# Cross-attention of a hybrid decoder step: the query layout moved ahead of the prompt scores, and a second prompt output product moved behind the exponential

## The chip, the cores and the metric

One core of one Trainium2 chip runs the whole kernel as one program. The metric is the device time of one execution in microseconds (us); of several runs the median is shown. Engines are named as the profile names them: PE is TensorE's matrix products, PEld its weight loads, DVE is VectorE, ACT is ScalarE, POOL is GpSimd, SP is SyncE. A "q" behind an engine's name means its queue of DMA issues.

## The reference

One inference step of one layer: two recurrent branches (SSD and GLA) merged by gates, cross-attention into 256 memory tokens, and a convolutional FFN. The same weights serve one prompt of 256 tokens and a group of 8 samples with 4 tokens each. All is float32. The change lies in the cross-attention:

```python
def _cross_attend(hn, mem_k, mem_v, w_cq, w_co):
    Bsz, L, _ = hn.shape
    q = (hn @ w_cq).reshape(Bsz, L, CROSS_HEADS, CROSS_HEAD_DIM).astype(jnp.float32)
    s = jnp.einsum('blhd,bmhd->bhlm', q, mem_k.astype(jnp.float32)) * (CROSS_HEAD_DIM ** -0.5)
    pr = jax.nn.softmax(s, axis=-1)
    o = jnp.einsum('bhlm,bmhd->blhd', pr, mem_v.astype(jnp.float32)).astype(hn.dtype)
    return o.reshape(Bsz, L, D_MODEL) @ w_co
```

There are 4 heads of 512 channels. The prompt (one row of 256 tokens) attends to keys and values that the kernel made earlier; each of the 8 samples attends to its own cached 256 keys and values per head.

## The kernel before

Activations stand transposed: 128 channels on the partitions, 288 tokens (256 of the prompt, 32 of the samples) along the free axis. Every weight matrix is loaded in pieces and split into a high and a low part: `whi` by ACT (L98), `wlo` by DVE (L100). Each product of full precision is then three products (high by high, high by low, low by high: L150, L151, L154). A **step** of a projection takes two blocks of 128 input channels and 256 output channels: one `whi`, one `wlo` and 12 products. Five pairs of `whi` and `wlo` are buffered, so ACT and DVE make them up to five steps ahead of PE.

The cross-attention is woven from two generators (L1591 to L1593). The main one is the query projection of the **next** head, 16 steps (`q_proj`, L1386); for the last head it is 12 steps of the output projection `w_co`. The other one is `attend(hd)` (L1430), the attention of the present head, cut into pieces by `yield`. `weave(main, bg, n_main, n_bg)` (L175) writes one main step, then so many pieces of `attend` that after main step i, counted from 0, `(i+1)*25//16` pieces have been written (`(i+1)*25//12` for the last head); what is left of `attend` after the last main step is written at once (`run(bg)`, L183). `attend` has 25 pieces. Through the text, "step 5" is the main step with i=5.

The pieces of `attend` in order, with their line numbers:

1. and 2. two times: four turns of the prompt's keys on PE (L1380), then their split into `kTh` (ACT, L190) and `kTl` (DVE, L191)
3. and 4. two times: `prompt_scores` (12 products of `qh`, `ql` by `kTh`, `kTl`: L1454, L1455, L1456), the prompt's softmax (L1359 to L1364), and two `turn`s of the samples' keys (`kT` from `kc`, DVE, L1419)
5. issue of the other four key loads (`keys`, POOL, L1405); the query layout: 16 products with the identity that spread the samples' queries `qsm` (L1493), and 8 copies on ACT into `xq` (L1498)
6. the split of the prompt's values into `vph` (ACT) and `vpl` (DVE)
7. and 8. sample scores of the first four samples (`la` from `kT`, `xq`, L1446), two times 64 products
9. turns of the prompt's probabilities (L1510), their split, one `turn`
10. to 13. three `turn`s, and behind them the prompt output products 0, 1 and 2 (`prompt_out`, six products each, L1468 to L1470, split into `co`)
14. and 15. issue of the value loads, and the sample scores of the other four samples
16. to 18. the maximum over the samples' scores (L1531 to L1544), and the exponential on ACT (`pu`, L1548)
19. prompt output product 3
20. the sums of the exponentials (L1553) and the probabilities (`rs`, `pu`, DVE, L1368 and L1370)
21. their turns on PE (L1558) and the copies into `pms` (DVE, L1560)
22. and 23. sample outputs, in two halves of 16 products (L1568): first those that read `vc`, then those that read `vq`
24. the copy `os` (ACT, L1572)
25. the products that sum the `os` rows by sample (L1576) and the split into `co`

Loads of cached keys and values and of the prompt's keys and values go through POOL's queue (`cache`, L1402): each is issued behind the one before it, and waits until the third before it has landed. Keys, late values and the prompt's keys and values share five buffers (`x4`, L1323), so the first keys `kc` of a head can be loaded only when the sample outputs of the head before have read its `vc`. A `turn` is placed behind the last `wlo` that has been written when it is written (L1418).

The order of writing is a priority, not the order on an engine: a planner places each instruction on its engine when it takes it to be ready, by its own estimates, earliest written first. The order on each engine is then fixed in the program. So a turn `kT` can be placed ahead of work that was written earlier, and main products stand between two products of `attend`.

Of the kernel before, what the change touches and what calls it, by code (L numbers as in the profile page):

```python
# [20 lines left out]
NB = 8  # L21
# [19 lines left out]
def hybrid_step(ctx: ExitStack, tc: tile.TileContext, I: dict, O: list):  # L41
# [14 lines left out]
    def acc_tile():  # L56
        return ps.tile([P, 512], F32, tag="acc", bufs=4, name="acc")

    def mm_tile():
        return ps.tile([P, 512], F32, tag="mm", bufs=3, name="mm")  # L60
# [128 lines left out]
    def split(hi, lo, src):  # L189
        S.copy(hi, src)  # L190
        V.tensor_tensor(lo, src, hi, ALU.subtract)  # L191
# [1133 lines left out]
    def k4(name):  # L1325
        return px.tile([P, 4, 256], F32, tag="k4", bufs=4, name=name)

    def r4(name):
        return px.tile([P, 4, 256], F32R, tag="r4", bufs=2, name=name)
# [4 lines left out]
    def v2(name):  # L1334
        return r4(name).rearrange("p d m -> p (d m)").rearrange("p (m d) -> p m d", m=2)
# [21 lines left out]
    def softmax(src, n, out):  # L1357
        mx = px.tile([P, 1], F32, tag="mx", bufs=3, name="mx")
        V.tensor_reduce(mx[0:n], src, axis=AX.X, op=ALU.max)  # L1359
        V.tensor_scalar(mx[0:n], mx[0:n], -SC, None, ALU.mult)  # L1360
        sm = px.tile([P, 1], F32, tag="sm", bufs=3, name="sm")
        S.activation(out, src, ACT.Exp, scale=SC, bias=mx[0:n], accum_out=sm[0:n])
        V.reciprocal(sm[0:n], sm[0:n])
        V.tensor_scalar(out, out, sm[0:n], None, ALU.mult)  # L1364
# [9 lines left out]
    def transpose_half(kv, d2):  # L1374

        a = mm_tile()
        for d in range(2):
            for m in range(2):
                dd = 2 * d2 + d
                TR(a[:, d * 256 + m * P:d * 256 + (m + 1) * P], kv[:, m, dd * P:(dd + 1) * P], ident)  # L1380
        return a.rearrange("p (d m) -> p d m", m=256)
# [29 lines left out]
    def rows_of(src, spread=False):  # L1411
        t = x4("kc" if spread else "vc")
        cache(t, src.rearrange("(p m) d -> p m d" if spread else "(m p) d -> p m d", p=P))
        return t

    def turn(kc):
        t = k4("kT").rearrange("p d m -> p (d m)")
        with tc.issue_after(last_lo[0].ins):  # L1418
            V.transpose(t, kc.rearrange("p s d -> p (s d)"))  # L1419
        return t.rearrange("p (s x c) -> p x s c", s=2, c=32)  # L1420

    def keys(hd, b):
        return rows_of(I["cache_mem_k"][b, :, hd, :], True)
# [6 lines left out]
    def attend(hd):  # L1430
# [3 lines left out]
        kc, kT, vc = [], [], []  # L1434
# [14 lines left out]
        def prompt_scores(l):  # L1449
            a = mm_tile()  # L1450
            ls = slice(l * P, (l + 1) * P)
            for d in range(4):
                qh, ql = (x[:, d % 2, ls] for x in qps[hd][d // 2])
                MM(a[:, 0:256], qh, kh[:, d, :], start=(d == 0), stop=False)  # L1454
                MM(a[:, 0:256], qh, kl[:, d, :], start=False, stop=False)  # L1455
                MM(a[:, 0:256], ql, kh[:, d, :], start=False, stop=(d == 3))  # L1456
            return a

        def prompt_softmax(a):
            pp = px.tile([P, 256], F32, tag="prp", bufs=2, name="prp")  # L1460
            softmax(a[:, 0:256], P, pp)
            return pp

        def prompt_out(d):
            a = mm_tile()
            ds_ = slice(d * P, (d + 1) * P)
            for m in range(2):
                MM(a[:, 0:SEQ], vh[:, m, ds_], pTh[:, m, :], start=(m == 0), stop=False)  # L1468
                MM(a[:, 0:SEQ], vh[:, m, ds_], pTl[:, m, :], start=False, stop=False)
                MM(a[:, 0:SEQ], vl[:, m, ds_], pTh[:, m, :], start=False, stop=(m == 1))  # L1470
            split(*(x[:, 0:SEQ] for x in co(4 * hd + d)), a[:, 0:SEQ])
# [6 lines left out]
        for d2 in range(2):  # L1478
            a = transpose_half(kp, d2)
            split(kh[:, 2 * d2:2 * d2 + 2, :], kl[:, 2 * d2:2 * d2 + 2, :], a)  # L1480
            yield
        prs = []
        for l in range(2):
            a = prompt_scores(l)
            prs.append(prompt_softmax(a))
            kT += [turn(kc[2 * l]), turn(kc[2 * l + 1])]
            yield
        for b in range(4, NB):
            kc.append(keys(hd, b))
        a = mm_tile()  # L1490
        for e in range(4):
            for i in (3, 2, 1, 0):
# [2 lines left out]
        for i in range(4):  # L1495
            r = slice(32 * i, 32 * i + 32)
            for q in range(2):
                S.copy(xq[r, :, :, 32 * q + 4 * i:32 * q + 4 * i + 4],  # L1498
                       a[r].rearrange("p (x q j l) -> p q x j l", q=2, j=4, l=NL)[:, q])
        yield  # L1500
        vh, vl = v2("vph"), v2("vpl")
        split(vh, vl, vp)
        yield
# [3 lines left out]
        a = mm_tile()  # L1507
# [8 lines left out]
        for d in range(3):  # L1516
            kT.append(turn(kc[5 + d]))
            yield
            prompt_out(d)
        yield  # L1520
        for b in range(4, NB):
            vals(b)
# [4 lines left out]
        for half in range(2):  # L1527
# [19 lines left out]
        su = px.tile([P, 1], F32, tag="sm", bufs=3, name="su")  # L1547
        S.activation(pu.rearrange("p (c s) -> p s c", s=2), ssc[:, 0:64].rearrange("p (s c) -> p s c", s=2), ACT.Exp,  # L1548
                     scale=SC, bias=mb, accum_out=su)
        yield  # L1550
        prompt_out(3)
        yield
# [3 lines left out]
        a = mm_tile()  # L1556
# [17 lines left out]
        a = mm_tile()  # L1574
# [16 lines left out]
    for hd in range(4):  # L1591
        main = q_proj(hd + 1) if hd < 3 else chain(steps(wo[0], 6), steps(wo[1], 6))
        weave(main, attend(hd), 16 if hd < 3 else 12, 25)  # L1593
# [164 lines left out]
    a = acc_tile()  # L1758
    fr = pf.tile([P, 3], F32, name="fr")
    b = acc_tile()  # L1760
# [65 lines left out]
```

## Time and profile before

| | |
|---|---|
| median of 3 runs | 2580.44 us (2579.44 to 2588.53) |
| profiled execution | 2577.89 us, span of its instructions 2576.1 us |
| granted TensorE clock, mean | 0.997 |
| PE busy | 2549.1 us (99%) |
| PEld busy | 2452.3 us (95%) |
| DVE busy | 1710.9 us (66%) |
| ACT busy | 1362.2 us (53%) |
| POOL busy | 298.7 us (12%) |
| DMA | 527.70 MB, mean 205 GB/s |

PE is busy nearly throughout, but this busy time is modelled: products overlap in it, and a stretch in which PE waits shows only as idle time in front of an instruction. So single waits are read from the lists of waits and from the instructions in order of time, not from the share. The cross-attention with its woven projections runs from about 1447 to 1636 us of the span, 47 to 50 us for each of the first three heads, 43.5 us for the last.

### The profile page before, as it was taken

The page shows a single profiled execution, that of the slowest core. Times are in us where ns is not written, and L with a number is a line of the kernel's source. Part 1 is how long each engine was busy: PE and PEld are TensorE (multiplying, and loading weights), DVE is VectorE, ACT ScalarE, POOL GpSimd, SP SyncE. Part 2 cuts the span into 40 slices and gives each one's busy share as a digit, 9 for nine tenths or more (in the row PEclk, how much of TensorE's full clock was granted, in tenths as well). Part 3 has the DMA queues.
Part 4 walks back from the last instruction along what each step waited for, and adds up shares of the span by engine and source line. Part 5 has one row for each costly group of instructions (what it writes and reads, how often), then busy time and mean ns, then how long its engine had stood idle before and what let it go on. Part 6 is the DMA issues. An engine that isn't in the chain of part 4 may idle for free. (4 is left out here: it accounts for less than half of the span.)

```text
span 2576.1 us, 51724 instructions
## 1 busy us (share of the span) xinstructions
PE 2549.1 (99%) x19781; PEld 2452.3 (95%) x19781; DVE 1710.9 (66%) x3647; ACT 1362.2 (53%) x2785; POOL 298.7 (12%) x388
## 2 busy tenths in 40 slices
PE   9999999999999999999999999999999999999998
PEld 7889999999999999999999988999999999999998
DVE  6656778667656666566676656567767576675765
ACT  7655566556553545454555534455545454454545
POOL 2002000000000000000110222202202021120200
PEclk9999999999999999999999999999999999999999
DMA  8666666766477857676876788845555555555553
GB/s 269 207 224 204 201 199 189 214 202 210 150 246 242 261 182 249 206 241 215 274 237 206 258 292 273 248 156 164 164 168 171 168 161 170 169 161 181 170 169 127
DMA packets 456724, 527.70 MB, mean 205 GB/s; under 512 B 23384, under 2 KB 401672, under 8 KB 456412
## 3 DMA queue, kind: packets, MB, share of 16 engines
q1 hardware_dynamic: 432780, 444.89, 53.9%
q0 software_dynamic: 23424, 79.24, 9.3%
q8 instruction: 155, 2.54, 0.4%
q14 instruction: 93, 0.76, 0.1%
q10 hardware_dynamic: 272, 0.26, 0.0%
HBM read 472.05 MB, written 52.26 MB: 204 GB/s over the span
## 5 line engine op out<-in xcount | busy, mean ns | idle before, releaser
L98 ACT CAST whi<-raw 128x512 fp32r<-128x512 f32 (+1 forms) x1464 | 897.2, 618 | 1039.5 <-PE acc L151 790.8
L100 DVE TENSOR_TENSOR wlo<-raw,whi 128x512 fp32r<-128x512 f32 (+1 forms) x1464 | 988.0, 687 | 686.3 <-ACT whi L98 666.6
L150 PE MATMUL acc<-xn,whi 128*128 128x288 f32 (+1 forms) x1936 | 552.1, 300 | 0.0
L151 PE MATMUL acc<-xn,whi 128*128 128x288 f32 (+1 forms) x1936 | 540.4, 295 | 0.0
L154 PE MATMUL acc<-xn,wlo 128*128 128x288 f32 (+1 forms) x1936 | 412.2, 294 | 0.1
L151 PE MATMUL acc<-hf,whi 128*128 128x288 f32 x1408 | 394.5, 296 | 0.0
L150 PE MATMUL acc<-hf,whi 128*128 128x288 f32 x1408 | 393.7, 294 | 0.0
L150 PEld LDWEIGHTS acc<-xn,whi 128*128 128x128 f32 (+1 forms) x1936 | 363.7, 188 | 11.8 <-issue 8.3
L151 PEld LDWEIGHTS acc<-xn,whi 128*128 128x128 f32 (+1 forms) x1936 | 364.1, 188 | 4.0 <-issue 2.9
L154 PEld LDWEIGHTS acc<-xn,wlo 128*128 128x128 f32 (+1 forms) x1936 | 310.1, 188 | 0.7 <-DVE wlo L100 0.6
L154 PE MATMUL acc<-hf,wlo 128*128 128x288 f32 x1408 | 298.5, 293 | 0.0
L151 PEld LDWEIGHTS acc<-hf,whi 128*128 128x128 f32 x1408 | 265.1, 188 | 0.0
L150 PEld LDWEIGHTS acc<-hf,whi 128*128 128x128 f32 x1408 | 264.6, 188 | 0.0
L154 PEld LDWEIGHTS acc<-hf,wlo 128*128 128x128 f32 x1408 | 226.0, 188 | 0.0
L1645 POOL COPY fsp<-fst 128x16 f32<-128x16 f32 x88 | 126.3, 1437 | 664.2 <-ACT fca L1651 366.7
L150 PE MATMUL acc<-pr,whi 128*128 128x288 f32 x704 | 196.8, 295 | 0.8 <-ACT whi L98 0.8
L151 PE MATMUL acc<-pr,whi 128*128 128x288 f32 x704 | 196.9, 295 | 0.0
L154 PE MATMUL acc<-pr,wlo 128*128 128x288 f32 x704 | 148.7, 292 | 0.0
L150 PE MATMUL acc<-un,whi 128*128 128x288 f32 x512 | 147.7, 304 | 0.1
L151 PE MATMUL acc<-un,whi 128*128 128x288 f32 x512 | 143.0, 295 | 0.0
L150 PEld LDWEIGHTS acc<-pr,whi 128*128 128x128 f32 x704 | 132.2, 188 | 1.0 <-ACT whi L98 1.0
L151 PEld LDWEIGHTS acc<-pr,whi 128*128 128x128 f32 x704 | 132.4, 188 | 0.0
(544 smaller groups left out, 4146.9 us busy)
## 6 DMA issues: line engine op xcount, KB each, us to landing
raw<-in_w_in_dram SPq DMA_DIRECT2D x240, 512.0 KB
raw<-in_w_up_dram SPq DMA_DIRECT2D x176, 512.0 KB
raw<-in_w_down_dram SPq DMA_DIRECT2D x88, 512.0 KB
raw<-in_w_cv_dram SPq DMA_DIRECT2D x32, 512.0 KB
raw<-in_w_ssd_out_dram SPq DMA_DIRECT2D x32, 512.0 KB
sin<-in_state_gla_dram POOLq DMA_DIRECT2D x32, 512.0 KB, 5.6
out_dram<-sin SPq DMA_DIRECT2D x32, 512.0 KB
raw<-in_w_gla_out_dram SPq DMA_DIRECT2D x32, 512.0 KB
```

The costliest lines, as they stand in the source:

```text
L98: S.copy(hi, raw)
L100: last_lo[0] = V.tensor_tensor(lo, raw, hi, ALU.subtract)
L150: MM(a, hi[:, k, cs], xh, start=(k0 + s0 + k == 0), stop=False)
L151: MM(a, hi[:, k, cs], xl, start=False, stop=False)
L154: MM(a, lo[:, k, cs], xh, start=False, stop=(k0 + s0 + k == nk - 1))
L1645: G.tensor_copy(sp[:, :, 0:2], st.rearrange("p (b k) -> p b k", k=2))
```

## The change

Two moves in `attend`; no instruction is added or taken away.

The query layout (the former piece 5 without the key loads) is written before the two prompt scores, as piece 3, so it stands between the turns of the prompt's keys and the prompt scores. Both prompt scores with their softmax and their turns of sample keys become pieces 4 and 5. The four key loads open the piece of the value split.

Prompt output product 2 is taken out of the loop and written behind the exponential, just ahead of product 3, with a `yield` of its own between exponential and product. The piece that held product 2 is now empty, so `attend` has 26 pieces, while `n_bg` stays 25: the 26th is written by `run(bg)`.

By the formula of `weave` the pieces then fall to the main steps as follows (heads 0 to 2):

| written behind main step | before | after |
|---|---|---|
| 0 | key turns 0 | key turns 0 |
| 1 | key turns 1, prompt scores 0 | key turns 1, query layout |
| 2 | prompt scores 1 | prompt scores 0 |
| 3 | query layout, value split | prompt scores 1, value split |
| 4 to 6 | sample scores, probabilities' turns | the same |
| 7 | output products 0 and 1 | output products 0 and 1 |
| 8 | output product 2, sample scores | sample scores |
| 9 to 11 | sample scores, maximum, exponential | the same |
| 12 | output product 3, sums | output products 2 and 3 |
| 13 | turns of the probabilities | sums |
| 14 | both halves of the sample outputs | turns of the probabilities, first half of the sample outputs |
| 15 | `os`, sums by sample | second half, `os`, sums by sample |

For the last head (12 main steps) the prompt scores 0 stand behind step 1 in both, now with the query layout ahead of them; prompt scores 1 move from step 1 to 2; sums and turns of the probabilities stand together behind step 10, and all of the sample outputs, `os` and the sums by sample behind step 11.

```diff
             a = transpose_half(kp, d2)
             split(kh[:, 2 * d2:2 * d2 + 2, :], kl[:, 2 * d2:2 * d2 + 2, :], a)
             yield
-        prs = []
-        for l in range(2):
-            a = prompt_scores(l)
-            prs.append(prompt_softmax(a))
-            kT += [turn(kc[2 * l]), turn(kc[2 * l + 1])]
-            yield
-        for b in range(4, NB):
-            kc.append(keys(hd, b))
         a = mm_tile()
         for e in range(4):
             for i in (3, 2, 1, 0):
...
                 S.copy(xq[r, :, :, 32 * q + 4 * i:32 * q + 4 * i + 4],
                        a[r].rearrange("p (x q j l) -> p q x j l", q=2, j=4, l=NL)[:, q])
         yield
+        prs = []
+        for l in range(2):
+            a = prompt_scores(l)
+            prs.append(prompt_softmax(a))
+            kT += [turn(kc[2 * l]), turn(kc[2 * l + 1])]
+            yield
+        for b in range(4, NB):
+            kc.append(keys(hd, b))
         vh, vl = v2("vph"), v2("vpl")
         split(vh, vl, vp)
         yield
...
         for d in range(3):
             kT.append(turn(kc[5 + d]))
             yield
-            prompt_out(d)
+            if d < 2:
+                prompt_out(d)
         yield
...
                      scale=SC, bias=mb, accum_out=su)
+        yield
+        prompt_out(2)
         yield
         prompt_out(3)
         yield
```

## The prediction

> **What bounds the kernel now.** I read the page first, then the waits of PE and its weight loads in the stage of the cross-attention, then the waits of DVE and ACT there, then the instructions in order of time around one border between heads.
>
> ```profile
> span 2576.1 us, 51724 instructions
> PE 2549.1 (99%) x19781; PEld 2452.3 (95%) x19781; DVE 1710.9 (66%) x3647; ACT 1362.2 (53%) x2785; POOL 298.7 (12%) x388
> ```
>
> PE bounds the kernel. A change that neither adds nor removes a product can only move the time by the waits of PE. So the question is how much PE waits in this stage (1425 to 1640 us), and for whom. The list of waits, weight loads first, then one row of the products; the columns are total us, times, longest:
>
> ```profile
> PEld mm L1454 <- ACT kTh L190: 5.0, 3, 2.0
> PEld mm L1455 <- DVE kTl L191: 4.4, 4, 1.2
> PEld mm L1553 <- ACT pu L1548: 1.8, 2, 1.7
> PEld mm L1576 <- ACT os L1572: 1.6, 1, 1.6
> PEld la L1446 <- ACT xq L1498: 1.0, 3, 0.3
> ...
> PE la L1446 <- ACT xq L1498: 1.7, 1, 1.7
> ```
>
> The prompt scores wait 5.0 + 4.4 = 9.4 us for the split of the prompt's keys, the sample scores 1.0 + 1.7 = 2.7 us for the query layout, the sums of the exponentials 1.8 us for the exponential. These 13.9 us, 0.54% of 2577.9, are what the change can reach.
>
> Why the split is late shows at the border from head 0 to head 1 (PE, POOL, DVE, ACT in order of time; start, length, and in brackets the idle time before it and who ended it):
>
> ```profile
> 1488.64 1.93 PE L1568 MATMUL la<-vc,pms 128*32 128x512 f32 x16
> 1490.38 1.90 PE L1568 MATMUL la<-vq,pms 128*32 128x512 f32 x16
> 1493.91 0.97 PE L1576 MATMUL mm<-fold,os 128*128 128x32 f32 x8
> 1496.38 0.60 PE L1380 MATMUL mm<-ident,vc 128*128 128x128 f32 x4
> 1498.39 0.60 PE L1380 MATMUL mm<-ident,vc 128*128 128x128 f32 x4
> 1500.79 0.39 PE L1454 MATMUL mm<-kTh,qh 128*128 128x256 f32 x1 [1.79 <-ACT kTh L190]
> 1502.17 0.39 PE L1455 MATMUL mm<-kTl,qh 128*128 128x256 f32 x1 [1.00 <-DVE kTl L191]
> 1508.39 1.08 PE L1493 MATMUL mm<-qsm,ident 128*32 128x128 f32 x32
> ...
> 1490.85 2.16 POOL L1405 DMA_DIRECT2D kc<-in_cache_mem_k_dram  x3 [6.61 <-PE la L1568]
> 1497.84 0.72 POOL L1405 DMA_DIRECT2D kc<-in_cache_mem_k_dram  x1 [4.83 <-DMA kc<-in_cache_mem_k_dram]
> ...
> 1489.19 0.69 DVE L100 TENSOR_TENSOR wlo<-raw,whi 128x512 fp32r<-128x512 f32 x1 [0.76 <-ACT whi L98]
> 1497.31 1.25 DVE L1419 STREAM_TRANSPOSE kT<-kc 128x1024 f32<-128x1024 f32 x1 [7.43 <-DMA kc<-in_cache_mem_k_dram]
> 1498.48 0.38 DVE L1395 TENSOR_TENSOR qs<-acc,rstd 128x256 f32<-128x256 f32 x1
> 1500.31 1.23 DVE L1419 STREAM_TRANSPOSE kT<-kc 128x1024 f32<-128x1024 f32 x1
> 1501.47 0.65 DVE L191 TENSOR_TENSOR kTl<-mm,kTh 128x512 fp32r<-128x512 f32 x1
> 1502.05 1.22 DVE L1419 STREAM_TRANSPOSE kT<-kc 128x1024 f32<-128x1024 f32 x1
> 1503.19 0.65 DVE L191 TENSOR_TENSOR kTl<-mm,kTh 128x512 fp32r<-128x512 f32 x1
> 1503.77 1.22 DVE L1419 STREAM_TRANSPOSE kT<-kc 128x1024 f32<-128x1024 f32 x1
> ...
> 1498.90 0.83 ACT L190 CAST qh<-qs 128x256 fp32r<-128x256 f32 x2 [3.71 <-DVE qs L1395]
> ```
>
> The chain: the first half of the sample outputs frees the buffers (1490.6), POOL issues the new keys (1490.85), the first lands 6.5 us later; its turn `kT` was placed on DVE ahead of the query scaling `qs` and holds DVE for 7.43 us. So `qs` is late, behind it `qh` on ACT, behind that `kTh`; and a second turn stands ahead of `kTl`. It is the same at all three borders:
>
> ```profile
> DVE kT L1419 <- DMA kc<-in_cache_mem_k_dram: 20.4, 3, 7.4
> ACT qh L190 <- DVE qs L1395: 11.3, 4, 3.7
> ```
>
> **The change part by part.**
>
> *Prompt scores behind the layout.* A main step is about 1.6 us: the two starts of L1380 are 2.0 us apart, less four turns for which I take 0.4. Between the second key turns and the prompt scores there now lie the layout (1.08 us) and one more step, 2.7 us. In head 0, whose keys are loaded early, only `kTl` is waited for; I take a quarter of 4.4, 1.1 us, and it goes: **-1.1**. The other three borders hold 9.4 - 1.1 = 8.3 us, 2.8 each.
>
> There the sample outputs move as well. The first half now has to wait for `pms`, and half a main step can be placed ahead of it, so the last `qs` become ready before the new keys are even asked for; I expect `qs` and `qh` ahead of the turn. I count from the issue of the first key (t = 0). PE leaves the first half at t = -0.3; then half a step 0.8, second half 1.8, step 0 1.6, sums by sample 0.8, turns 0.4, step 1 1.6, turns 0.4, layout 1.1, step 2 1.6: the prompt scores could start at t = 9.8. DVE gets the first key at 6.5. If three turns (1.2 each) stand ahead of the first `kTl` (0.65), it is done at 10.8 and 1.0 to 1.1 us of waiting are left; the second `kTl`, 11.4, comes just as the products that need it do. If only one or two turns stand ahead, nothing is left. If the fourth turn stands ahead of the second `kTl`, much is left (the second rival). I take 1.1 for each border, nearest to the row order in which turns and `kTl` alternate but with DVE free earlier: 8.3 - 3.3, **-5.0** (ends -8.3 and +5).
>
> *Layout earlier.* Its copies on ACT:
>
> ```profile
> 1460.88 0.62 ACT L98 CAST whi<-raw 128x512 fp32r<-128x512 f32 x1 [2.21 <-DMA raw<-in_w_cq_dram]
> 1461.41 2.55 ACT L1498 COPY xq<-mm 32x256 f32<-32x256 f32 x8
> ```
>
> They take 2.55 us, and in head 0 stood behind a `whi` that waited for a weight load. Now two prompt scores and two more steps lie between layout and sample scores. **-2.7** (ends -2.7 and 0). The copies now stand on ACT ahead of the exponentials of the prompt's softmax; those follow the prompt scores, a step later than the layout, so nothing waits.
>
> *Two products behind the exponential.* The 1.8 us come nearly all from the end of head 2:
>
> ```profile
> 1581.07 0.62 ACT L98 CAST whi<-raw 128x512 fp32r<-128x512 f32 x1 [4.53 <-DMA raw<-in_w_co_dram]
> 1581.59 0.31 ACT L1548 ACTIVATE pu<-la,mb 128x64 f32<-128x64 f32 x1
> ...
> 1582.04 0.38 PE L1553 MATMUL mm<-su,total 128*128 128x1 f32 x2 [1.46 <-ACT pu L1548]
> ```
>
> The sums now come a whole step (1.6 us) and six products later: **-1.8** (ends -1.8 and 0, if the weight load is later by as much). The place that product 2 leaves needs no cover: nothing waited there.
>
> *Everything behind it is a piece later.* Turns of the probabilities and first half of the sample outputs now stand together in heads 0 to 2, as they do now in the last head:
>
> ```profile
> 1627.69 0.38 PE L1558 MATMUL mm<-ident,pu 128*128 128x128 f32 x2
> 1628.80 1.92 PE L1568 MATMUL la<-vc,pms 128*32 128x512 f32 x16
> ...
> 1628.11 0.49 DVE L1560 COPY pms<-mm 128x128 f32<-128x128 f32 x2 [0.90 <-PE mm L1558]
> ```
>
> From turns to outputs 1.1 us pass, 0.9 without the turns themselves, and in this row no wait is left because half a main step stands between. I take 0.1 a head, **+0.3** (ends 0.3 and 2.7). In the last head no main product is left at that place: **+0.9** (ends 0 and 0.9). The copy `os` and the sums by sample now follow the second half directly in heads 0 to 2; the next head's step 0 can stand between, so 0 (other end 1.6 each, the row of `os` above, 4.8). In the last head that wait of 1.6 us stays.
>
> *Moves that cost nothing.* The four later key loads are written behind the prompt scores, but POOL can issue them only when turns have freed buffers, so they keep their time. The prompt's softmax is a step later; two steps and the sample scores still lie ahead of its turns on PE. The split of product 2 moves from step 8 to 12 and is read by `w_co` only after the last head. The value split keeps its step. If key loads were late after all, their turns would hold DVE; that is in the bounds above.
>
> *The clock.* Once in this stage it falls, in the last head (share of the granted clock behind POOL's column):
>
> ```profile
> 1596.40:1599.80 3.40, 1.66 (x12) 1.36 (x12) 3.40 (x6) 1.79 (x4) 0.90 (x2) 1.00 0.86 240
> 1599.80:1603.20 3.40, 3.40 (x18) 3.40 (x17) 2.35 (x5) 0.44 (x1) 1.10 (x2) 0.51 0.82 302
> ```
>
> After 3.4 us with PE busy for 1.66, 18 products start in the next 3.4 us, where 28 would at 0.12 us each: 1.2 us lost. One row gives no threshold, so I put 0 in the sum and -1.2 among the bounds. [...]
>
> **Sum.** -1.1 - 5.0 - 2.7 - 1.8 + 0.3 + 0.9 = -9.4 us. The profiled execution took 2577.9 us (its span 2576.1 and 1.8 around it), 2.5 under the median of 2580.4; 2577.9 - 9.4 = 2568.5, against the median 2571.0. That is -0.36%.
>
> **The rivals.**
>
> *All waits go.* The split is never waited for, and the clock does not fall: -9.4 - 3.3 - 1.2 = -13.9, 2566.5. For it: 2.7 us of new cover against waits of 2.8. Against: DVE has nothing to do before 6.5, and then everything at once.
>
> *The fourth turn stands ahead of the second `kTl`* (this one ends slower). DVE keeps its order, and a turn whose key has not landed holds all behind it, as the 7.43 us above show. The fourth turn ran at 1503.77, t = 12.9; were it ahead of the second `kTl`, that would be done at 14.8, and the prompt scores would wait some 4.4 us at each border, 13.2 in place of 8.3: +4.9. With the other terms (-1.1 - 2.7 - 1.8 + 1.2) +0.5; with both `kTl` behind it 5.1 each, +2.6, 2583.0. It decides from t = 12.6 for the second `kTl` on, where 2.8 us are waited as now. For it: DVE is free earlier than before, so a turn can be taken earlier. Against: before, the fourth came last.
>
> *The new waits are not filled.* `pms` and `os` are waited for in heads 0 to 2 in full: 2.4 + 4.8 = +7.2 on the sum, -2.2, 2578.2. Against it: half a step stands at 1627.69. [...]
>
> *The first turn still stands ahead of `qs`* (the change doesn't do what it says). Then the layout waits for `qsm`: DVE has it at about 8.7, PE comes at 7.1, so 1.6 to 1.9 us are lost at each border instead of 2.8: -2.7 to -3.6 in place of -5.0, about -7.5, 2573.
>
> **Chances.** Forecast 0.42 (alone 2568 to 2574: nothing left, or 2 us, at each border); all waits go 0.12; fourth turn 0.25; not filled 0.09; first turn 0.12. Range 2566.5 to 2582.5, from all waits gone to the fourth turn's case. 0.5%, 12.9 us, is about what a measurement of this kernel tells from no change. Faster by more needs all waits gone: 0.13. Slower by more would need three times what the slow rival costs: 0.04. Within: 0.83.
>
> **What would show it.** The waits of L1454 for `kTh` gone; those of L1455 for `kTl` at some 3 us; L1446 no longer waiting for `xq`, L1553 not for `pu`. On DVE `qs` ahead of the first `kT` of heads 1 to 3, and the wait for `kc` shorter than 20.4. Half a step between L1558 and L1568. A clock of 1.00 in the last head would add to the gain. Wrong would be: a `kT` waiting for `kc` directly ahead of a `kTl`, idle time ahead of L1493 for `qsm`, or ahead of L1568 and L1576 in heads 0 to 2.

## The result, and the profile after

| | before | after |
|---|---|---|
| median of 6 runs each, us | 2583.80 (2579.44 to 2588.53) | 2567.75 (2566.84 to 2573.91) |
| ratio to before, 95% interval | | 0.9946 (0.993 to 0.9961) |
| profiled execution, us (span) | 2577.89 (2576.1) | 2566.84 (2565.1) |

The kernel is 0.54% faster. A second measurement of both kernels on another chip gave 2569.16 us and 0.9958 (0.9942 to 0.9974). The forecast was 2571.0 us with a range of 2566.5 to 2582.5.

The two profiled executions differ by 11.0 us. Where they differ shows when the stage is cut at the first main product of each head's first step, by head: 47.1, 47.8, 49.7 and 43.5 us before, together 188.1; 43.9, 44.6, 44.6 and 45.3 after, together 178.4. So 9.6 us come from the stage. The cut does not fall at the same work in both kernels: before, a head's eight sums by sample (L1576, 0.8 us) stand ahead of it, after the change behind it, so they count with the next head (589 products against 582 in head 0). Counted with their own head, the changed kernel takes 44.7, 44.6, 44.6 and 44.5 us: the first three heads gained 10.6 us, and the last head lost 1.0. The rest of the 11.0 us lies in other parts, which vary by a few us from run to run (the first product of the stage starts between 1447.3 and 1451.6 us in the runs shown here). The table by stretches, first before, then the changed kernel; columns are length, busy time and number of instructions of PE, PEld, DVE, ACT and POOL, then granted clock, DMA share and GB/s:

```profile
1447.60:1494.70 47.10, 44.79 (x589) 39.84 (x588) 29.20 (x60) 20.09 (x44) 11.55 (x16) 1.00 0.79 268
1494.70:1542.50 47.80, 44.90 (x590) 39.94 (x589) 30.15 (x61) 19.74 (x44) 13.01 (x18) 1.00 0.83 284
1542.50:1592.20 49.70, 45.34 (x590) 39.99 (x589) 30.34 (x61) 19.62 (x44) 12.99 (x18) 1.00 0.82 280
1592.20:1635.70 43.50, 40.59 (x542) 35.11 (x541) 27.07 (x53) 16.92 (x39) 11.93 (x18) 0.96 0.81 271
...
1447.40:1491.30 43.90, 43.81 (x582) 38.82 (x580) 32.40 (x67) 20.25 (x45) 12.27 (x17) 1.00 0.87 291
1491.30:1535.90 44.60, 44.60 (x591) 39.79 (x587) 30.96 (x61) 20.25 (x44) 12.96 (x18) 1.00 0.90 306
1535.90:1580.50 44.60, 44.60 (x591) 39.77 (x587) 30.73 (x61) 19.83 (x44) 13.05 (x19) 1.00 0.88 309
1580.50:1625.80 45.30, 40.77 (x551) 35.81 (x547) 25.47 (x45) 17.01 (x38) 11.89 (x18) 0.96 0.77 264
```

In heads 0 to 2 of the changed kernel PE has next to no idle time left. The last head has 4.5 us, where it was 2.9 before, and a clock of 0.96 in both. The waits of the stage after the change, products first, then weight loads, then DVE and ACT:

```profile
PE mm L1469 <- DVE pTl L191: 3.3, 1, 3.3
PE mm L1579 <- ACT os L1575: 0.7, 1, 0.7
...
PE mm L1454 <- DVE kTl L191: 0.2, 1, 0.2
...
PEld mm L1469 <- DVE pTl L191: 3.6, 1, 3.6
PEld mm L1579 <- ACT os L1575: 1.6, 1, 1.6
PEld mm L1454 <- DVE kTl L191: 0.4, 1, 0.4
PEld la L1571 <- DVE pms L1563: 0.2, 1, 0.2
...
DVE kT L1419 <- DMA kc<-in_cache_mem_k_dram: 12.0, 7, 3.1
ACT qh L190 <- DVE qs L1395: 4.8, 4, 1.4
```

(L1579 is L1576 of before, L1571 is L1568, L1485 is L1493, L1556 is L1553.) The 9.4 us at the prompt scores are down to 0.4, the waits for `xq` and for the exponential are gone from the list. A new one of 3.6 us has come: the output products wait for `pTl`, the low part of the prompt's probabilities.

The border from head 0 to head 1, PE, POOL and DVE in order of time:

```profile
1485.45 0.38 PE L1561 MATMUL mm<-ident,pu 128*128 128x128 f32 x2
1486.60 1.92 PE L1571 MATMUL la<-vc,pms 128*32 128x512 f32 x16
1489.44 1.92 PE L1571 MATMUL la<-vq,pms 128*32 128x512 f32 x16
...
1488.81 2.16 POOL L1405 DMA_DIRECT2D kc<-in_cache_mem_k_dram  x3 [6.88 <-PE la L1571]
...
1489.55 0.42 DVE L1395 TENSOR_TENSOR qs<-acc,rstd 128x256 f32<-128x256 f32 x1 [1.29 <-PE acc L154]
1493.59 1.25 DVE L1419 STREAM_TRANSPOSE kT<-kc 128x1024 f32<-128x1024 f32 x1 [2.58 <-DMA kc<-in_cache_mem_k_dram]
1494.94 1.23 DVE L1419 STREAM_TRANSPOSE kT<-kc 128x1024 f32<-128x1024 f32 x1
1496.66 0.68 DVE L191 TENSOR_TENSOR kTl<-mm,kTh 128x512 fp32r<-128x512 f32 x1
```

`qs` now stands ahead of the first turn, which still waits for its key (2.58 us), but with nothing urgent behind it. Between the two halves of the sample outputs, and between turns and outputs, lie halves of a main step: 1.1 us from L1561 to L1571 as in the last head of before.

The new wait lies in the last head, DVE, PE and POOL in order of time, and then the clock:

```profile
1600.91 1.25 DVE L1419 STREAM_TRANSPOSE kT<-kc 128x1024 f32<-128x1024 f32 x1 [3.14 <-DMA kc<-in_cache_mem_k_dram]
1602.08 0.65 DVE L191 TENSOR_TENSOR pTl<-mm,pTh 128x512 fp32r<-128x512 f32 x1
...
1602.78 0.39 PE L1469 MATMUL mm<-pTl,vph 128*128 128x256 f32 x1 [3.32 <-DVE pTl L191]
...
1592.73 0.72 POOL L1405 DMA_DIRECT2D kc<-in_cache_mem_k_dram  x1 [3.38 <-DVE wlo L100]
...
1600.40:1603.80 3.40, 1.02 (x8) 1.02 (x9) 2.67 (x3) 0.12 (x1) 1.04 (x2) 1.00 0.37 92
1603.80:1607.20 3.40, 3.40 (x30) 3.12 (x32) 2.28 (x6) 1.25 (x3) 1.85 (x3) 0.50 0.69 241
```

The turn of a later key stands ahead of `pTl`, its key was asked for at 1592.73 and lands at 1600.8. It is the mechanism of the old border, at another place. The last head lost only 1.0 us by it, as its old waits for `kTh`, `kTl` and `xq` (1.0, 1.2 and 0.3 us) went at the same time.

### The profile page after: what moved, and what is told of

Same layout as the page of the kernel before. It is cut to its first block, busy times and chain, and to the rows that moved or that the text cites. A ratio compares the mean times of both kernels' runs of the same rounds, so it can differ in the third digit from the quotient of the medians.

```text
span 2565.1 us, 51729 instructions
## 1 busy us (share of the span) xinstructions
PE 2544.5 (99%) x19781; PEld 2448.4 (95%) x19781; DVE 1713.6 (67%) x3647; ACT 1363.7 (53%) x2785; POOL 300.0 (12%) x388
## 4 chain that ended last, share of the span: by engine, by line
PE 96%; DMA 1%; DVE 1%; ACT 0%; issue 0%; DVEq 0%; ACTq 0%
PE acc L150 27%; PE acc L151 27%; PE acc L154 27%; PE acc L376 2%; PE acc L377 2%; PE acc L380 2%; PE la L1178 1%; PE la L1446 1%; PE mm L1186 1%; PE mm L878 1%; DMA kc<-in_cache_mem_k_dram 1%; PE mm L1151 1%; PE la L1571 1%; DMA raw<-in_w_in_dram 0%; DMA raw<-in_w_cv_dram 0%; PE mm L890 0%
```

## The experiments

All numbers of a stage are sums of its four heads, cut as above (before 188.1 us, after 178.4), each of one profiled execution; the times and ratios are medians. Ratios are to the kernel before on the same chip. The theory under test, "shift": the borders are freed not by the layout's cover but because the extra piece pushes the sample outputs into the last step.

**The layout alone.** Output product 2 stays in its loop and there are 25 pieces.

```diff
-            if d < 2:
-                prompt_out(d)
+            prompt_out(d)
...
-        yield
-        prompt_out(2)
```

> Only the query layout is moved; output product 2 stays in its loop and attend has 25 pieces, so the sample outputs keep their place behind step 14. Theory 'shift' (the borders are freed because the sample outputs now fall into the last step, so the query scaling qs comes ahead of the first key turn on DVE): the first turn still stands ahead of qs and waits about 7 us for its key at each border; the layout itself (L1493) now waits 1 to 2 us for qsm at each border; the sample scores no longer wait for xq (-2.7), head 0 gains 1; the exponential's 1.8 us stay; in all -5 to -7 us. Rival 'cover' (the 2.7 us of layout and step between turns and scores hide the split, wherever qs stands): all of the 9.4 and 2.7 us go, the exponential's 1.8 stay: -11 to -12 us, no wait at the layout.

2574.82 us, ratio 0.9979 (0.997 to 0.9989); stage 185.1 us, so 3.0 gained.

```profile
PE mm L1485 <- DVE co L191: 4.1, 3, 1.6
DVE kT L1419 <- DMA kc<-in_cache_mem_k_dram: 24.5, 4, 7.9
...
1495.99 1.25 DVE L1419 STREAM_TRANSPOSE kT<-kc 128x1024 f32<-128x1024 f32 x1 [7.93 <-DMA kc<-in_cache_mem_k_dram]
1497.16 0.39 DVE L1395 TENSOR_TENSOR qs<-acc,rstd 128x256 f32<-128x256 f32 x1
```

As "shift" has it: the turn is ahead of `qs` and waits 7.93 us, and the layout waits for `qsm` at all three borders. (The list names `co` on DVE, the instruction counted last; `qsm` stands just ahead of it.) Most of the wait was moved from the prompt scores to the layout. The stage's gain is smaller than either theory said, because two more waits came, 2.6 us for `pTl` and 2.5 for `vq`; the median fell by 5.3 us, within the range of "shift". "Cover" expected 11 to 12 us and is out. One thing that both theories expected failed: the 1.8 us for the exponential did not stay, 0.2 were left, though nothing new stands between it and its sums.

**The product alone.** The layout stays, product 2 moves, 26 pieces.

> Only output product 2 is moved behind the exponential; the layout stays behind the prompt scores; 26 pieces. 'Shift': qs ahead of the first turn at all three borders, the waits for kTh gone, DVE's wait for kc down from 20 to about 10 us; but the prompt scores follow the key turns directly, so waits of 1 to 3 us for kTl stay at each border; the exponential's 1.8 us go; the waits for xq stay; -3 to -6 us. 'Cover': the 9.4 us at the prompt scores stay, only the 1.8 go: -1 to -2 us.

2575.35 us, ratio 0.9983 (0.997 to 0.9996); stage 182.2, so 5.9 gained.

```profile
PEld mm L1455 <- DVE kTl L191: 4.9, 6, 1.7
DVE kT L1419 <- DMA kc<-in_cache_mem_k_dram: 8.0, 3, 3.3
```

The waits for `kTh` are gone (0.2 us left) without the layout's move; what is left is 4.9 us for `kTl`, because the prompt scores follow the key turns directly. This is what the layout's place covers.

**Both moves without the empty piece.**

```diff
         for d in range(3):
...
                 prompt_out(d)
-        yield
         for b in range(4, NB):
             vals(b)
```

> Both moves, but the yield that leaves an empty piece is taken out, so attend has 25 pieces and everything from the sums of the exponentials on falls to the steps of before. 'Shift': the first turn stands ahead of qs again, L1485 waits 1 to 2 us for qsm at each border; -6 to -8 us, with the kc waits of DVE back near 7 us each. 'Cover': as the changed kernel, -10 to -12 us.

2570.73 us, ratio 0.9965 (0.9955 to 0.9976); stage 183.8, so 4.3 gained.

```profile
PE mm L1485 <- DVE co L191: 3.2, 2, 2.0
DVE kT L1419 <- DMA kc<-in_cache_mem_k_dram: 24.3, 5, 8.3
```

With 25 pieces the first turn blocks DVE again, though both moves are in. The rows decide for "shift". The time doesn't: the median is 9.4 us under the kernel before, between the two theories' figures and not to be told from the changed kernel's second measurement (0.9958, 0.9942 to 0.9974), while the stage's gain is under both. The profiled execution took 3.6 us more than the median, so its stage may not be a typical one. How much of the whole gain is lost without the empty piece stays open.

**The empty piece alone.** One more line in the kernel before:

```diff
                      scale=SC, bias=mb, accum_out=su)
         yield
+        yield
         prompt_out(3)
```

> Neither move: the order of before, with one more yield (an empty piece) ahead of output product 3, so that everything from product 3 on comes a piece later. 'Shift': qs ahead of the first turn at the borders, waits for kTh gone, some kTl waits of 1 to 3 us stay; -2 to -6 us. 'Cover': nothing, 0 within 2 us, with the 9.4 us at the prompt scores in place.

2574.93 us, ratio 0.9978 (0.9966 to 0.9989); stage 182.3, so 5.7 gained.

```profile
PEld mm L1455 <- DVE kTl L191: 4.2, 6, 1.1
DVE kT L1419 <- DMA kc<-in_cache_mem_k_dram: 7.6, 5, 2.7
...
1495.20 0.42 DVE L1395 TENSOR_TENSOR qs<-acc,rstd 128x256 f32<-128x256 f32 x1 [1.24 <-PE acc L154]
1498.98 1.25 DVE L1419 STREAM_TRANSPOSE kT<-kc 128x1024 f32<-128x1024 f32 x1 [2.31 <-DMA kc<-in_cache_mem_k_dram]
```

A `yield` with no work in it brings 5.7 of the 9.6 us (5.2 us by the medians). Counted as above, heads 1 to 3 gain 7.7; head 0 loses 1.9 us, with PE idle for 2.6 us ahead of its sample scores, where it was 1.7 before. Shift and layout together bring the rest: the one frees DVE, the other covers what is left.

**The changed kernel again,** for comparison with the next three.

> The changed kernel itself, for comparison on the same chip. Stage of the cross-attention about 178.4 us in its four heads, with one wait of some 3.5 us for pTl in the last head and a clock of one half for 3.4 us behind it.

2569.16 us; stage 179.0, last head 44.7. The wait for `pTl` is there (2.8 us), and the clock fell twice, behind that wait and just behind the end of the stage (1627.1 us); its mean over the execution is 0.997, in the first profile 0.998.

**Turns 5 to 7 behind `pTl`.**

```diff
-            kT.append(turn(kc[5 + d]))
+            kT.append(turn(kc[5 + d], pl))
```

Here `pl` is the instruction that writes `pTl`, and `turn` is issued behind it.

> The changed kernel with turns 5 to 7 of the sample keys placed on DVE behind pTl in every head. Theory 'late turn' (the wait in the last head comes from a turn placed ahead of pTl whose key has not landed, and the clock falls because PE idled): the wait of 3.5 us at L1469 goes, the clock stays at 1.00 through the stage, -3.5 to -5 us in the last head against the changed kernel (41 to 42 us instead of 45.3), heads 0 to 2 within 0.5 us. Rival 'late probabilities' (pTl is late because the softmax of the prompt now ends a step later): the wait stays at 1 us or more. Rival 'clock for itself': the wait goes and the half clock stays at about the same place, -3.5 us only.

2570.80 us, ratio 0.996 (0.9947 to 0.9973); stage 182.3, last head 46.8. The wait for `pTl` is gone, and nothing is gained:

```profile
1624.44 3.64 PE L1571 MATMUL la<-vq,pms 128*32 128x512 f32 x16 [2.81 <-DMA vq<-in_cache_mem_v_dram]
...
1618.06 0.72 POOL L1405 DMA_DIRECT2D vq<-in_cache_mem_v_dram  x1 [2.10 <-DMA vq<-in_cache_mem_v_dram]
...
1620.30:1623.70 3.40, 1.33 (x16) 0.13 (x4) 0.63 (x1) 0.00 (x0) 0.00 (x0) 0.99 0.80 275
1623.70:1627.10 3.40, 2.66 (x16) 0.60 (x16) 0.00 (x0) 0.00 (x0) 0.00 (x0) 0.50 0.09 32
```

PE now waits at the second half of the sample outputs for the last value load, and the clock is halved behind that, 0.50 for 10.2 us (1623.7 to 1633.9). No theory expected this: the wait went, as "late turn" said, but its gain didn't come. The wait for `pTl` was only where a later limit showed first. Head 1 also lost 1.9 us, waiting 1.7 for `pms`, behind an ACT that waited for a weight load.

**Four loads in flight.**

```diff
-        if len(asked) >= 3:
-            tc.add_manual_dep(d.ins, asked[-3].ins.name,
+        if len(asked) >= 4:
+            tc.add_manual_dep(d.ins, asked[-4].ins.name,
```

> The changed kernel with four loads of the cache in flight instead of three. In the last head the third of the later key loads was issued at 1592.73 us, just behind the landing of the prompt's values (1592.17), the third load before it; its buffer was free at 1589.7. 'Late turn': with four, that key is asked for 2 to 3 us earlier and lands before its turn is due, the wait for pTl falls under 1 us although the order on DVE is the same, -2.5 to -4.5 us. Rival 'DMA is full' (loads only share the same rate): every load takes longer, the key lands no earlier, the wait stays, or moves to the sample outputs.

2566.24 us, ratio 0.9951 (0.9933 to 0.997); stage 177.4, last head 41.2. There three turns ahead of `pTl` run through without a wait,

```profile
1601.30 3.48 DVE L1419 STREAM_TRANSPOSE kT<-kc 128x1024 f32<-128x1024 f32 x3
```

and the mean granted clock of the execution is 0.998, where it was 0.996 with turns 5 to 7 behind `pTl`. Heads 0 to 2 take 0.8, 0.9 and 1.5 us more than in the changed kernel's first profile (0.3, 0.8 and 0.7 more than in its second), with waits for `pms` at L1571 in head 1 and for `pu` at L1561 in head 2.

**Layout and empty piece, product 2 back in its loop.**

> The changed kernel with product 2 back in its loop and an empty piece ahead of product 3, so the layout is moved and everything from product 3 on comes a piece later. Theory 'the product itself is worth nothing': borders as in the changed kernel, no wait at L1553 for the exponential in head 2, since the sums already fall a step later; heads 0 to 2 within 0.7 us of the changed kernel. Rival 'product 2 covers the exponential': a wait of 1 to 1.6 us for pu at L1553 in head 2.

2567.78 us, ratio 0.9951 (0.9935 to 0.9968); stage 175.9: 44.0, 44.6, 44.6, 42.7. No wait for `pu` at the sums of the exponentials. Heads 0 to 2 are those of the changed kernel within 0.1 us, so once the empty piece is there, the move of product 2 adds nothing to it. The clock is halved at 1628.3 us, just behind the stage (it ends at 1627.4), so that loss is not in the 175.9.

**Four loads in flight in the last head only,** on the changed kernel. A variable `depth`, 3 and from the last head on 4, stands in place of the 3.

> The changed kernel with four cache loads in flight in the last head only, three in the others. Theory 'load chain' (the last head, with 12 steps instead of 16, is bound by its chain of loads, three at a time, and pTl or vq is only where it shows): heads 0 to 2 as in the changed kernel (43.9 to 45.3 us), the last head 41 to 42.5 us instead of 44.7 to 45.3, no wait over 1 us but those for os and co at its end; 3 to 4 us under the changed kernel, some 2564 us. Rival 'DMA is full': the last head stays over 44 us, or loses 2 us at L1571 for vq.

2564.44 us, ratio 0.9932 (0.9918 to 0.9945); stage 174.4: 43.6, 44.6, 46.1, 40.1. The longest product waits of the whole stage, as far as their releaser is known:

```profile
PE mm L1488 <- DVE co L191: 0.8, 1, 0.8
PE mm L1582 <- ACT os L1578: 0.7, 1, 0.7
...
```

(L1488 is the layout, L1582 the sums by sample.) Two more waits are of 0.4 us and less. The last head is 5.2 us shorter than in the changed kernel (4.6 than in its second profile), and the mean granted clock of the execution is 0.999, against 0.998 and 0.997 in those two. Head 2 is longer than expected, 46.1 us, with the wait at the layout in it. This is the fastest median of those tried. By the ratios, each on its own chip, it is 0.26% under the second measurement of the changed kernel, but the two intervals overlap slightly (0.9945 against 0.9942), so that it is faster than the changed kernel is likely and not shown.

**The same with product 2 in its loop.**

> Product 2 back in its loop, layout moved, all from product 3 on a piece later, and four loads in flight in the last head. 'Load chain': last head 41 to 42.5 us instead of 42.7, stage 174 to 175 us in its four heads against 188 before, 2563 to 2566 us. If product 2 behind the exponential is worth something, it is slower than the kernel with it by over 1 us.

2565.03 us, ratio 0.9941 (0.9929 to 0.9954); stage 174.3, last head 40.2. Not to be told from the kernel with the product moved.

**Turns behind the query's last split,** in the kernel before, with no move at all.

```diff
-            kT += [turn(kc[2 * l]), turn(kc[2 * l + 1])]
+            kT += [turn(kc[2 * l], ql), turn(kc[2 * l + 1], ql)]
```

> The kernel before with one thing changed: the four turns of the first sample keys stand on DVE behind the query's last split. No move, 25 pieces. Theory 'order on DVE' (the prompt scores waited because the first turn, whose key was late, stood ahead of qs): the waits for kTh at the three borders go (1.9, 1.9 and 0.9 us), DVE's longest wait for a key falls from 7.4 to 4 us or less, some 1 us or less is left for kTl; -4 to -8 us, about as the empty piece alone (-5.7 in the stage). Rival 'cover is needed': the waits for kTh turn into longer waits for kTl, 2 us or more at each border, and the gain is under 2 us.

2575.69 us, ratio 0.9976 (0.9966 to 0.9985); stage 184.7. The edit moves the line numbers by one to three: L1456 is L1454 of before, L1457 is L1455, L1448 is L1446.

```profile
PEld mm L1456 <- ACT kTh L190: 0.2, 1, 0.2
PEld mm L1457 <- DVE kTl L191: 2.3, 5, 1.0
PEld la L1448 <- ACT xq L1501: 3.9, 3, 3.1
```

The 9.4 us at the prompt scores fall to 2.5: the order on DVE was the cause. Heads 1 and 2 gain 2.6 and 3.3 us. But PE waits 2.9 us in head 0 and again in head 3 ahead of the sample scores, in head 0 the clock is halved behind that (1468.9 us), and head 0 loses 2.1. So the stage gains 3.4, less than was expected, and the median 4.9, just within it.

**Four loads in the last head, on the kernel before.**

> The kernel before with four cache loads in flight in the last head only. Theory 'next bound' (the chain of loads binds the last head only once the prompt scores no longer wait): nothing in heads 0 to 2, the last head 42 to 43.5 us with the waits for kTh and kTl in place, 0 to -2 us in all. Rival 'the loads were the bound all along': the last head falls to 40 to 41.5 us, as in the changed kernel with four loads, -3 us or more.

2582.85 us, ratio 1.0014 (1.0003 to 1.0026); last head 48.2.

```profile
PEld mm L1455 <- ACT kTh L190: 6.7, 3, 2.6
PEld mm L1556 <- ACT pu L1551: 2.8, 1, 2.8
```

No gain, and in the last head a loss of 4.7 us that no theory expected: a wait for the exponential (L1556 here is the sums' product; the exponential stood on ACT behind a `whi` that waited 4.3 us for its weight load) and two halvings of the clock, at 1601.26 and 1631.98 us, where there was one before. So the loads were not the bound before; they are the next one, behind the waits that the change takes away. In heads 0 to 2, with three loads as before, this kernel took 46.0, 48.3 and 49.9 us, together 0.4 less than before. Whether the late weight load comes from the fourth load in flight was not tested.

## Why the prediction was right, and where it was off

The sum said -9.4 us on the profiled execution; the stage gave -9.6 and the execution -11.0. Term by term, by the weight loads' waits:

- *Prompt scores, -1.1 and -5.0 with 3.3 left.* The mechanism was right: `qs` ahead of the turn, because half a main step comes ahead of the sample outputs. The size was off: 0.4 us are left, not 3.3. Two inputs failed. The first key took 4.8 us from issue to turn (1488.81 to 1493.59), where 6.5 was taken from the row of before; and two turns, not three, stood ahead of the first `kTl`. The term measured is -9.0.
- *Layout, -2.7, and exponential, -1.8.* Both waits are gone, but the reason given for the second, "two products behind the exponential", was half wrong. The step between does without the products (no wait with product 2 in its loop). And the wait goes with a weight load that ACT waits for ahead of the exponential: with the layout alone, and with the turns behind the query's split, 0.2 us were left with neither products nor step. So that the change took these 1.8 us away is not shown.
- *Turns and `pms`, +0.3.* 0.2 measured. *The last head, +0.9:* not there. The last main step was split around the turns, so half of it was left to fill the wait. *`os`, 0:* right, half of the next head's step 0 stands there.
- *Moves that cost nothing.* This is the step that failed. The prompt's probabilities are turned after a later softmax, and the turns of the later keys stand ahead of `pTl`; in the last head one of these had not landed. The text left this to the bounds and looked for it at the borders only. The prediction had nothing for this in its sum; it cost 3.6 us.
- *The clock, 0.* The halving did not go away, it moved from 1599.8 to 1603.8, behind the new wait, and took 3.41 us at both places.

So two errors of about 3 us, one each way, cancelled in the sum: that the forecast came out within 0.2 us of the stage is luck, while the main mechanism, `qs` ahead of the turn, was right. The slow rival, a turn whose key has not landed holding all behind it, came true at another place than the one for which it was priced.

The median came out lower than forecast, 2567.75 against 2571.0. 1.6 of these 3.3 us are the stage and the parts outside it in the profiled run; the rest is that the runs shown before lay 2.5 us over the profiled one, and those after only 0.9.

Two details of the prediction need a correction. The upper end of its range, 2582.5, lies under the 2583.0 that it prices itself for the fourth turn ahead of both `kTl`. The 0.5% that it takes as the least that a measurement tells is too coarse: the intervals here reach 0.1 to 0.2% to each side.

## What to carry to other kernels

Where two streams of work are woven, ask of each piece what it frees, not only what it computes: an empty piece gained 5.7 us of the stage by moving the point at which a buffer came free against the point at which the other stream's results were due. An instruction that waits for a load should stand behind everything on its engine that is ready: with the layout alone a turn waited 7.93 us for its key, and `qs` started only behind it, at 1497.16. But when one such wait goes, look at the whole chain of loads behind it before counting the gain, because in the last head the wait only moved from `pTl` to `vq`. And a depth of prefetch that is right where the steps are many can be too small where they are few: a fourth load in flight shortened only the last head, from 45.3 to 40.1 us, and only once the earlier waits were gone (on the kernel before it took 48.2 us instead of 43.5).

## What the runs showed of the hardware

In the kernel before and in the changed one the granted clock fell once in the stage, to 0.50 for 3.41 us, at 1599.8 and at 1603.8 us. In the kernel before, the products of the prompt scores start 0.12 us apart ahead of the fall (1599.20 and 1599.32) and 0.21 us apart in it (1600.17 and 1600.38).

PE did not stand idle for the whole 3.4 us ahead of these halvings: it was modelled busy for 1.66 us (before) and 1.02 us (after). Nor does the modelled busy time alone tell where the clock is halved. In the kernel before, the 3.41 us from 1497.44 us on hold 1.61 us, and the clock stayed at 1.00 in them and in the 3.41 us behind; with layout and empty piece, it was 0.50 behind 3.4 us that hold 2.34. First before, then layout and empty piece:

```profile
1497.44:1500.85 3.41, 1.61 (x14) 1.38 (x12) 3.37 (x9) 1.93 (x5) 1.44 (x2) 1.00 0.65 195
1500.85:1504.26 3.41, 2.41 (x17) 2.17 (x18) 3.41 (x5) 0.89 (x2) 1.45 (x2) 1.00 0.85 259
...
1624.90:1628.30 3.40, 2.34 (x18) 1.84 (x15) 0.29 (x1) 0.85 (x2) 2.67 (x5) 1.00 0.39 119
1628.30:1631.70 3.40, 3.40 (x17) 3.40 (x16) 0.71 (x2) 0.62 (x1) 3.31 (x7) 0.50 0.97 312
```

The stretch of 2.34 us is at the end of the last head, with the wait for `os` in it (0.7 us), in good part with products of 32 columns; whether that matters was not tested. The empty piece alone has the same wait there, and the clock stayed at 1.00: from 1627.4 to 1630.8 us PE was modelled busy for 2.60 us, in the 3.4 us behind for 3.15.
